# Output projection in seven half-size block products instead of eight

## The chip, the cores and the metric

The kernel runs on one core of one Trainium2 chip. The metric is the device time of one execution in microseconds (us). TensorE (PE in the profile, its weight loads PEld) multiplies, VectorE (DVE), ScalarE (ACT) and GpSimd (POOL) work on tiles in the on-chip memory SBUF and in the accumulators PSUM, SyncE (SP) issues most DMAs. A tile has 128 partitions; "128x544" is 544 numbers in each.

## The reference

One layer of a decoder for a prompt of 1024 tokens and 64 sample tokens, 1088 in all, with 1024 features. The part around the change is:

```python
merged = g_r * (o_r @ lp["w_br_rwkv"]) + g_p * (o_p @ lp["w_br_pool"])
x = x + gt * (merged @ lp["w_out"])
sh, sc, gt = ada_mod(c, lp["w_ada_mlp"], lp["b_ada_mlp"])
h = rms_norm(x, lp["norm_mlp"]) * (1 + sc) + sh
x = x + gt * (jnp.square(jax.nn.relu(h @ lp["w_ff1"])) @ lp["w_ff2"])
```

`w_out` is 1024 x 1024. All data is float32. The gate `gt` has one value for each feature of the prompt, and one for each feature and each of the eight sample sequences.

## The kernel before, in words

Everything is kept with features in partitions and tokens in columns: eight row blocks of 128 features by 1088 columns. The columns are cut into two halves of 544 (`HF`) and four quarters of 272 (`HQ`). A float32 operand is split into a rounded part (`hi`, written by ScalarE) and what is left of it (`lo` = source - `hi`, a subtraction on VectorE or GpSimd); `mm3` then makes three matmuls, `hi*hi`, `hi*lo` and `lo*hi`, into one accumulator. Weights come as halves of a row block, 128x512, and go through `halves` (L236 for `whi`, L237 for `wlo`, which alternates between VectorE and GpSimd).

Three stages matter here. In the **merge stage** eight jobs `or_job(m)` (36 matmuls of 362 or 364 columns each) multiply by `w_br_rwkv`; VectorE multiplies each PSUM result into the gate tile `t` (L1569), L1573 adds the pooling branch `u` (on GpSimd for m < 4, on VectorE above), and L1576 and L1577 split the merged row block into `hi` and `lo` halves, tiles `mr`. In the **output projection** sixteen jobs `out_job(m, i)`, one for each row block m and column half i, make 48 matmuls of 272 columns each, first the eight of the left half, then the eight of the right; each job has two fresh PSUM banks (`mm`, four exist), which VectorE reads once each: `residual` (L2132) multiplies by the gate and adds to the residual row `xr[m]`, a tile of the pool `hx`; in the last quarter the 64 sample columns go through `ns` (L2135) and a GpSimd addition (L2137). Then **the channel mixer** begins, whose first products need `norm2(0)`, the normed left half. Its parts are the squares (ScalarE), their sums (L1620), a matmul with ones, `rms`, the scaling L1635 and `parts` (L1606, L1607), which splits the result.

Each engine executes its instructions in the order in which they stand in the program. That order comes from `Pace.run`: the back program (the matmuls and what follows them directly) runs ahead, each matmul adding a computed time to a clock, and the side programs `norm2(0)`, `norm2(1)` and `ada` are let in when that clock has passed what their `yield` asks for, or when a condition in `self.done` holds. The tile framework puts the waits: a tile name with a limited number of buffers waits for the readers of the buffer's last use. `behind` copies one column from the tile `self.mark` into a new tile (GpSimd, L1536) before a DMA fills it, so that the DMA stays behind the work on `mark`; `next_row` does so for the rows of `x` that become `xr`.

The channel mixer already makes its products in seven blocks instead of eight (`pair_steps`, `product`).

## Time and profile before

| | us |
|---|---|
| time, median of 3 runs (lowest, highest) | 1586.95 (1586.65, 1593.05) |
| the profiled execution, its own time | 1586.22 |
| its span, first to last instruction | 1584.4 |
| PE busy in the span | 1550.8 (98%) |
| DVE busy | 1088.5 (69%) |
| ACT busy | 754.9 (48%) |
| POOL busy | 354.7 (22%) |
| mean granted TensorE clock | 0.998 |

All times in the trace count from the start of the span. In a row of a timeline the columns are start, time taken, engine, line, operation, output <- inputs, shapes and count, and in brackets the idle time before it with what ended that; successive instructions of one line stand in one row (x2), with their time together. In a row of grouped instructions stand the busy time of all, the mean of one in ns, and the idle time before them. In a table of windows each engine has its busy time and, in brackets, its count of instructions. L207 is the line of every matmul, so matmuls are told apart by their tiles.

### The profile page before, as it was taken

What the parts mean: (1) busy time and instruction counts of PE and PEld (TensorE: products, weight loads), DVE (VectorE), ACT (ScalarE), POOL (GpSimd) and SP (SyncE); (2) the same over time, 40 slices, a digit from 0 to 9 for tenths busy, and PEclk for the clock granted to TensorE, in tenths of its full rate; (3) what the DMA queues carried; (4) which work ended last, traced back from release to release, by engine and by line L of the source; (5) the groups of instructions that cost most, each with busy time, mean ns of one, the idle gap of its engine ahead of it and who ended that gap; (6) DMA issues with size and microseconds to landing.
All of it is one profiled execution on the core that took longest, in us unless ns stands there. A gap on an engine that the chain in (4) does not pass through costs nothing.

```text
span 1584.4 us, 35298 instructions
## 1 busy us (share of the span) xinstructions
PE 1550.8 (98%) x14153; PEld 1448.6 (91%) x14153; DVE 1088.5 (69%) x1868; ACT 754.9 (48%) x1543; POOL 354.7 (22%) x470
## 2 busy tenths in 40 slices
PE   7999999999999999999999999999999999999997
PEld 3899788998898789889989999999999999999997
DVE  4697777698488747557536776777455767786866
ACT  5454354355346434433335665554545765553323
POOL 3300100020002000103313223222233344521221
PEclk9999999999999999999999999999999999999999
DMA  9334322423423344937874466657667865573213
GB/s 340 108 108 156 129 87 88 143 94 133 130 100 109 101 137 153 337 121 278 286 267 149 155 212 209 220 201 266 214 213 284 274 198 187 194 285 132 94 41 113
DMA packets 124627, 279.21 MB, mean 176 GB/s; under 512 B 18112, under 2 KB 32448, under 8 KB 124464
## 3 DMA queue, kind: packets, MB, share of 16 engines
q1 hardware_dynamic: 109152, 228.52, 42.1%
q0 software_dynamic: 9264, 32.22, 6.2%
q10 hardware_dynamic: 6048, 16.23, 3.0%
q8 instruction: 111, 1.82, 0.5%
q14 instruction: 52, 0.43, 0.1%
HBM read 197.95 MB, written 78.95 MB: 175 GB/s over the span
## 4 chain that ended last, share of the span: by engine, by line
PE 82%; DVE 6%; DMA 5%; ACT 3%; issue 3%; POOL 1%; ACTq 0%; SPq 0%; DVEq 0%; POOLq 0%
PE mm L207 34%; PE pr L207 34%; PE w L207 7%; PE wc L207 6%; DMA aw<-in_w_ada_mix 2%; DMA wraw<-in_w_br 1%; DMA wrx<-in_w_out 1%; DVE hx L1938 0%; DMA x<-in_xT 0%; ACT whi L236 0%; DVE hx L1635 0%; DMA sraw<-in_w_in 0%; PE wc L214 0%; DVE e L419 0%; DVE wlo L237 0%
## 5 line engine op out<-in xcount | busy, mean ns | idle before, releaser
L207 PE MATMUL mm<-hx,whi 128*128 128x364 f32 (+1 forms) x1920 | 497.4, 340 | 1.0 <-POOL hx L539 1.0
L207 PEld LDWEIGHTS mm<-hx,whi 128*128 128x128 f32 x1920 | 332.1, 188 | 33.1 <-issue 17.5
L207 PE MATMUL pr<-mr,whi 128*128 128x272 f32 x1792 | 337.5, 288 | 0.2 <-DVE hx L1938 0.2
L207 PE MATMUL mm<-hx,wlo 128*128 128x364 f32 (+1 forms) x960 | 315.1, 328 | 0.0
L207 PEld LDWEIGHTS pr<-mr,whi 128*128 128x128 f32 x1792 | 280.5, 188 | 2.2 <-issue 2.1
L207 PE MATMUL pr<-mr,wlo 128*128 128x272 f32 x896 | 257.4, 287 | 0.0
L207 PEld LDWEIGHTS mm<-hx,wlo 128*128 128x128 f32 x960 | 180.6, 188 | 0.3 <-DVE wlo L237 0.2
L207 PE MATMUL pr<-hx,whi 128*128 128x272 f32 x896 | 170.7, 289 | 0.3 <-ACT hid L1742 0.3
L207 PEld LDWEIGHTS pr<-mr,wlo 128*128 128x128 f32 x896 | 168.8, 188 | 0.0
L207 PE MATMUL mm<-mr,whi 128*128 128x272 f32 (+5 forms) x736 | 152.5, 302 | 0.0
L236 ACT ACTIVATE whi<-wraw 128x512 fp32r<-128x512 f32 x127 | 79.8, 628 | 138.8 <-PE mm L207 41.5
L207 PEld LDWEIGHTS pr<-hx,whi 128*128 128x128 f32 x896 | 140.7, 189 | 1.4 <-issue 0.8
L236 ACT ACTIVATE whi<-wr 128x512 fp32r<-128x512 f32 x138 | 86.4, 628 | 111.8 <-PE pr L207 81.1
L207 PE MATMUL pr<-hx,wlo 128*128 128x272 f32 x448 | 129.2, 288 | 0.0
L237 DVE TENSOR_TENSOR wlo<-wraw,whi 128x512 fp32r<-128x512 f32 x117 | 84.9, 725 | 56.5 <-ACT whi L236 56.3
L207 PEld LDWEIGHTS mm<-mr,whi 128*128 128x128 f32 x736 | 119.1, 188 | 3.2 <-issue 2.7
L207 PE MATMUL mm<-mr,wlo 128*128 128x272 f32 (+5 forms) x368 | 110.2, 300 | 0.0
L237 DVE TENSOR_TENSOR wlo<-wr,whi 128x512 fp32r<-128x512 f32 x103 | 76.8, 748 | 14.8 <-ACT whi L236 14.6
L207 PE MATMUL pr<-t,whi 128*128 128x272 f32 x448 | 85.0, 288 | 0.0
L207 PEld LDWEIGHTS pr<-hx,wlo 128*128 128x128 f32 x448 | 84.3, 188 | 0.0
L594 DVE TENSOR_TENSOR px<-mm,rb 128x298 f32<-128x298 f32 (+2 forms) x100 | 50.5, 508 | 34.5 <-PE mm L207 33.9
L237 POOL TENSOR_TENSOR wlo<-wrx,whi 128x512 fp32r<-128x512 f32 x31 | 42.6, 1376 | 139.7 <-ACT whi L236 135.3
(494 smaller groups left out, 2864.4 us busy)
## 6 DMA issues: line engine op xcount, KB each, us to landing
wr<-in_w_ff SPq DMA_DIRECT2D x137, 256.0 KB, 3.4
hid<-d_ch POOLq DMA_DIRECT2D x72, 272.0 KB, 3.7
wraw<-in_w_in SPq DMA_DIRECT2D x62, 256.0 KB, 2.9
d_ch<-hx SPq DMA_DIRECT2D x52, 272.0 KB, 3.9
hid<-in_w_ada_mlp SPq DMA_DIRECT2D x24, 512.0 KB, 6.2
d_th<-px SPq DMA_DIRECT2D x22, 544.0 KB, 3.1
wt<-d_x SPq DMA_DIRECT2D x20, 544.0 KB, 4.6
wraw<-in_w_ff SPq DMA_DIRECT2D x36, 256.0 KB, 3.0
```

The lines of the kernel that those rows point to most:

```text
L207: return self.nc.tensor.matmul(out, lhsT, rhs, **kw)
L236: nc.scalar.activation(hi, raw, AF.Copy)
L237: (nc.gpsimd if pool else nc.vector).tensor_tensor(lo, raw, hi.bitcast(F32), op=ALU.subtract)
L594: self.nc.vector.tensor_tensor(out, ps[:, :m], self.rb[:, c0:c0 + m], op=ALU.mult)
```

## The change

The eight products of 2 x 2 blocks (weights and merged activations each cut in halves of their 1024 features and of their tokens) become seven, each a product of a sum of weight blocks and a sum of activation blocks. With B11, B12 the left and right token halves of the merged blocks m = 0 to 3, and B21, B22 those of m = 4 to 7, the seven activation operands are B11, B21, B22, t1 = B12 - B11, t2 = B22 - t1, t3 = t2 - B11 and t4 = B21 - t2. A product has four row blocks j, a step (c, j) is 24 matmuls of 272 columns, and the 28 steps of `out_steps` have 672 matmuls where the sixteen jobs had 768.

The accumulators are kept over several products: step (1, j) opens two banks O[j], and (6, j), (7, j) and (4, j) add to them; (5, j) opens two again, to which (3, j) adds; the four steps of product 2 share one pair, O[4], from the tag `w`. After every step `residual` (L2237) adds what the two banks hold, times the gate, to half of a residual row: 56 reads where there were 32.

The sums: `or_job` makes t1 on GpSimd (L1588) for m < 4; for m > 3 it subtracts in place t2 and t4 (L1598, L1599; GpSimd for m = 4 to 6, VectorE for 7); L1607 makes t3 in eight subtractions on GpSimd, taking `hi` and `lo` of B11 away from t2 in turn. Each is split by `halve` (L1539, L1540). Weight sums are made on GpSimd in `prep` (two subtractions for c = 6, one addition for c = 5, an addition and a subtraction for c = 3: 20 in all). There are 36 loads of w_out halves instead of 32, and 28 splits instead of 32.

`norm2(0)` takes its rows in the order in which they are finished, which is now before the last eight steps, (5, *) and (3, *), and its scaling (L1739) of six of the rows takes its factor from a copy (`behind_mark`, L1706 and L1707, GpSimd) that follows the row named by `mark`; four of its eight remainders (L1702) are on GpSimd instead of one. `next_row` runs two steps behind instead of five. Outside this stretch the constant table is loaded in three parts instead of two, with part of it freed after the first phase.

```diff
-        mg = [[], []]
...
+        Bq, mid, late = {}, {}, {}
+        def halve(c, k, src, place, pool=False):
+            hi, lo = Bq[c, k] = place()
+            nc.scalar.activation(hi, src, AF.Copy)
+            (nc.gpsimd if pool else nc.vector).tensor_tensor(lo, src, hi.bitcast(F32), op=ALU.subtract)
         def behind(x):
...
-            m = step - 5
+            m = step - SHIFT
...
             def after():
-                t = S["t"]
-                (nc.vector if m > 3 else nc.gpsimd).tensor_tensor(t, t, S["u"], op=ALU.add)
-                hi, lo = zip(*[MR() for _ in range(2)])
-                for i, s in enumerate(split):
-                    nc.scalar.activation(hi[i], t[:, s], AF.Copy)
-                    nc.vector.tensor_tensor(lo[i], t[:, s], hi[i].bitcast(F32), op=ALU.subtract)
-                mg[0].append(hi)
-                mg[1].append(lo)
-                self.mark = t
+                t, k = S["t"], m % 4
+                a, b = t[:, :HF], t[:, HF:]
+                for c in split if m == 7 else (slice(0, NT),):
+                    (nc.vector if m > 3 else nc.gpsimd).tensor_tensor(t[:, c], t[:, c], S["u"][:, c], op=ALU.add)
+                if m < 4:
+                    halve("11", k, a, MR)
+                    x = mid[k] = p.tile([P, HF], F32, tag="wr2", bufs=5, name=self.nm("mid"))
+                    nc.gpsimd.tensor_tensor(x, b, a, op=ALU.subtract)
+                    halve("t1", k, x, MR)
+                    self.mark = x
+                else:
+                    halve("21", k, a, MR)
+                    halve("22", k, b, MR)
+                    self.mark = Bq["22", k][0].bitcast(F32)
                 next_row(m)
+                if m > 3:
+                    eng, x = nc.gpsimd if m < 7 else nc.vector, mid[k]
+                    eng.tensor_tensor(b, b, x, op=ALU.subtract)
+                    eng.tensor_tensor(a, a, b, op=ALU.subtract)
+                    late[k] = a, b
+                if m == 7:
+                    for k in range(4):
+                        halve("t2", k, late[k][1], HXP)
+                    for k in range(4):
+                        b, (hi, lo) = late[k][1], Bq["11", k]
+                        for x in (hi, lo):
+                            nc.gpsimd.tensor_tensor(b, b, x.bitcast(F32), op=ALU.subtract)
                 self.done.add(("or", m + 4))
             return Job([io["w_br"][m][:, 0:512]], begin, after=after, xs=lambda: orr, tags=TG)
...
-        def out_job(m, i):
-            return Job([io["w_out"][m][:, h * 512:(h + 1) * 512] for h in range(2)], lambda: self.residual(self.xr[m], gt[:, m, :]), QH[i],
-                       ("mm", "mm"), lambda: out_done(m, i), lambda: mg)
+        def out_steps():
+            A = lambda m, h: io["w_out"][m][:, h * 512:(h + 1) * 512]
+            D, O = [{} for _ in range(4)], {}
+            sub = lambda o, x, y: nc.gpsimd.tensor_tensor(o, x, y, op=ALU.subtract)
+            add = lambda o, x, y: nc.gpsimd.tensor_tensor(o, x, y, op=ALU.add)
+            def raw(j, key, m, h):
+                self.nr += 1
+                t = D[j][key] = self.raw(self.nr % 7 == 6) if self.nr % 7 in (3, 6) else p.tile([P, 512], F32, tag="wr2", bufs=5, name=self.nm("wr2"))
+                nc.sync.dma_start(t, A(m, h))
+                return t
+            def prep(c, j):
+                d = D[j]
+                def go():
+                    if c < 3:
+                        t = self.raw(self.nw % 2)
+                        nc.sync.dma_start(t, A(j, c - 1))
+                        return self.halves(t, False)
+                    if c == 6:
+                        x, y, z = raw(j, "a", j, 0), raw(j, "b", j + 4, 0), raw(j, "c", j + 4, 1)
+                        sub(y, x, y)
+                        sub(x, z, y)
+                        return self.halves(x, False)
+                    if c == 7:
+                        return self.halves(d["b"], True)
+                    if c == 4:
+                        return self.halves(d["c"], False)
+                    if c == 5:
+                        y, z = raw(j, "b", j + 4, 0), raw(j, "c", j + 4, 1)
+                        add(y, y, z)
+                        return self.halves(y, False)
+                    x, z = raw(j, "a", j, 0), raw(j, "e", j, 1)
+                    add(x, x, z)
+                    sub(x, x, d["b"])
+                    return self.halves(x, False)
+                return go
+            def run(c, j):
+                key, m, i = {1: ("11", j, 0), 2: ("21", j, 0), 6: ("t2", j, 1), 7: ("t3", j + 4, 1), 4: ("t4", j + 4, 0),
+                             5: ("t1", j + 4, 1), 3: ("22", j, 1)}[c]
+                def go(w):
+                    if c in (1, 5) or (c, j) == (2, 0):
+                        tag = "w" if (c, j) in ((2, 0), (1, 2), (5, 1)) else "mm"
+                        O[4 if c == 2 else j] = [self.ps(tag) for _ in range(2)]
+                    ps = O[4 if c == 2 else j]
+                    for q in range(2):
+                        o, s = ps[q][:, :HQ], slice(q * HQ, (q + 1) * HQ)
+                        for k in range(4):
+                            xh, xl = Bq[key, k]
+                            self.mm(o, w[k][0], xh[:, s], start=k == 0 and c in (1, 2, 5), stop=False, skip_group_check=True)
+                            self.mm(o, w[k][0], xl[:, s], start=False, stop=False, skip_group_check=True)
+                            self.mm(o, w[k][1], xh[:, s], start=False, stop=k == 3, skip_group_check=True)
+                            yield
+                        self.residual(self.xr[m], gt[:, m, :])(i * HF + q * HQ, HQ, o)
+                    self.mark = self.xr[m]
+                    next_row(len(self.xr) + SHIFT)
+                    if c == 2 and j == 0:
+                        for k in range(4):
+                            halve("t3", k, late[k][1], HXP)
+                    if c == 2 and j == 3:
+                        for k in range(4):
+                            halve("t4", k, late[k][0], MR)
+                    self.done.add(("out", m, 2 if c == 1 else 3 if c in (6, 7) else i))
+                return go
+            two = lambda c, a: [(c, a), (c, a + 1)]
+            seq = [(1, 0), (2, 0), (1, 1), (2, 1)] + two(2, 2)
+            for a in (0, 2):
+                seq += (two(1, 2) if a else []) + two(6, a) + two(7, a) + two(4, a)
+            for a in (0, 2):
+                seq += two(5, a) + two(3, a)
+            return [(prep(c, j), run(c, j)) for c, j in seq]
...
+        def behind_mark(kb):
+            t = p.tile([P, 1], F32, tag="g3", bufs=8, name=self.nm("g3"))
+            nc.gpsimd.tensor_copy(t, self.mark[:, 0:1])
+            nc.gpsimd.tensor_copy(t, g2[:, kb, 0:1])
...
+            for n, m in enumerate((4, 5, 0, 1, 6, 7, 2, 3) if i else (0, 1, 4, 5, 2, 3, 6, 7)):
...
+                yield lambda: ("out", m, i) in self.done and (m > 3 or i or ("out", m, 2) in self.done)
...
-                for kb in (k, k + 4):
+                for kb in (2 * k, 2 * k + 1) if i == 0 else (k, k + 4):
...
-                        nc.vector.scalar_tensor_tensor(x[kb], x[kb], g2[:, kb, 0:1], r, op0=ALU.mult, op1=ALU.mult)
+                        nc.vector.scalar_tensor_tensor(x[kb], x[kb], behind_mark(kb) if kb in TIED else g2[:, kb, 0:1], r, op0=ALU.mult, op1=ALU.mult)
...
-                        parts(kb // 4, k, x[kb], kb == 7)
+                        parts(kb // 4, kb % 4, x[kb], kb in POOLK)
...
+        def out():
+            for _, run in osteps:
+                yield from run(made.pop(0))
+                more()
...
-        for i in range(2):
-            outs = [out_job(m, i) for m in range(8)]
...
-            for j in outs[0 if i else 2:]:
-                order += U(j)
...
+                yield from out()
...
+TIED = (2, 3, 4, 5, 6, 7)
+POOLK = (1, 3, 5, 7)
+SHIFT = 2
```

On VectorE, at the end of the merge stage and in the first steps of the projection, this stood before (`t_1274` is the last merged block, `mr` its halves, `hx` left of the arrow the residual rows, `mm` a bank of a job):

```order
L1577 TENSOR_TENSOR mr_1283_9425<-t_1274_9371,mr_1283_9425 128x544
L237 TENSOR_TENSOR wlo_1293_9470<-wraw_1291_9467,whi_1292_9469 128x512
L2132 SCALAR_TENSOR_TENSOR hx_1262_9306<-mm_1285_9433,gt1_8920,hx_1262_9306 128x272
L2132 SCALAR_TENSOR_TENSOR hx_1262_9306<-mm_1286_9434,gt1_8920,hx_1262_9306 128x272
L2132 SCALAR_TENSOR_TENSOR hx_1273_9368<-mm_1294_9473,gt1_8920,hx_1273_9368 128x272
L2132 SCALAR_TENSOR_TENSOR hx_1273_9368<-mm_1295_9474,gt1_8920,hx_1273_9368 128x272
```

and this stands at the same place now (`hx_1292` to `hx_1295` are the remainders of t2, `t_1281` the last merged block, `w_1306` and `w_1307` the pair of banks of product 2, `mm_1318` and `mm_1319` those of step (1, 1), `wlo_1305` the weight remainder of (1, 1); `hx_1235` and `hx_1247` are residual rows 0 and 1):

```order
L1540 TENSOR_TENSOR hx_1292_9461<-t_1248_9204,hx_1292_9461 128x544
L1540 TENSOR_TENSOR hx_1293_9464<-t_1259_9268,hx_1293_9464 128x544
L1598 TENSOR_TENSOR t_1281_9396<-t_1281_9396,mid_1245_9196 128x544
L1540 TENSOR_TENSOR hx_1294_9467<-t_1270_9332,hx_1294_9467 128x544
L2237 SCALAR_TENSOR_TENSOR hx_1235_9137<-w_1307_9527,gt1_8922,hx_1235_9137 128x272
L237 TENSOR_TENSOR wlo_1288_9445<-wrx_1286_9442,whi_1287_9444 128x512
L1599 TENSOR_TENSOR t_1281_9396<-t_1281_9396 128x544
L237 TENSOR_TENSOR wlo_1305_9523<-wraw_1303_9520,whi_1304_9522 128x512
L2237 SCALAR_TENSOR_TENSOR hx_1247_9201<-mm_1318_9581,gt1_8922,hx_1247_9201 128x272
L1540 TENSOR_TENSOR hx_1295_9470<-t_1281_9396,hx_1295_9470 128x544
L2237 SCALAR_TENSOR_TENSOR hx_1247_9201<-mm_1319_9582,gt1_8922,hx_1247_9201 128x272
L2237 SCALAR_TENSOR_TENSOR hx_1235_9137<-w_1306_9526,gt1_8922,hx_1235_9137 128x272
```

The read of `w_1306`, which step (2, 1) needs free, is the last of these rows; eight operations on two SBUF tiles and three reads of other banks stand ahead of it in these rows.

On GpSimd, at the same place, before:

```order
L237 TENSOR_TENSOR wlo_1281_9420<-wrx_1279_9417,whi_1280_9419 128x512
L1536 COPY hx_1284_9430<-t_1274_9371 128x1
L1536 COPY hid_1289_9440<-t_1274_9371 128x1
L1536 COPY hid_1290_9443<-t_1274_9371 128x1
L1536 COPY hid_1296_9499<-t_1274_9371 128x1
L1559 DMA hx_1284_9430<-in_xT 128x1088
```

and now (`wr2` are weight sums for product 6, `t_1248`, `t_1259`, `t_1270` and `t_1281` are t2 becoming t3, `hx_1302` is residual row 4 and `hx_1235` residual row 0):

```order
L1568 DMA hx_1291_9456<-in_xT 128x1088
L1622 TENSOR_TENSOR wr2_1326_9651<-wr2_1325_9649,wr2_1326_9651 128x512
L1607 TENSOR_TENSOR t_1248_9204<-t_1248_9204,mr_1215_9041 128x544
L1607 TENSOR_TENSOR t_1259_9268<-t_1259_9268,mr_1221_9068 128x544
L1545 COPY hx_1302_9517<-hx_1235_9137 128x1
L1607 TENSOR_TENSOR t_1270_9332<-t_1270_9332,mr_1232_9129 128x544
L1607 TENSOR_TENSOR t_1248_9204<-t_1248_9204,mr_1215_9041 128x544
```

The copy that opens residual row 4 reads a column of residual row 0 and stands behind the weight sum and the first two subtractions for t3; the next write of residual row 0, the last row of the VectorE list above, has to come after it.

On VectorE, at the scaling of `norm2(0)`, before (`mm_1383` and `mm_1394` are banks of jobs of the right half):

```order
L1635 SCALAR_TENSOR_TENSOR hx_1284_9430<-hx_1284_9430,g2_8921,t_1389_10138 128x544
L1635 SCALAR_TENSOR_TENSOR hx_1332_9738<-hx_1332_9738,g2_8921,t_1389_10138 128x544
L1635 SCALAR_TENSOR_TENSOR hx_1304_9543<-hx_1304_9543,g2_8921,t_1389_10138 128x544
L1635 SCALAR_TENSOR_TENSOR hx_1347_9830<-hx_1347_9830,g2_8921,t_1389_10138 128x544
L2132 SCALAR_TENSOR_TENSOR hx_1273_9368<-mm_1394_10157,gt1_8920,hx_1273_9368 128x272
L2132 SCALAR_TENSOR_TENSOR hx_1273_9368<-mm_1395_10158,gt1_8920,hx_1273_9368 128x208
```

and now (`mm_1440` and `mm_1441` are the banks of step (5, 2)):

```order
L1739 SCALAR_TENSOR_TENSOR hx_1258_9263<-hx_1258_9263,g3_1434_10497,t_1418_10379 128x544
L1723 TENSOR_TENSOR t_1188_8926<-t_1188_8926,t_1432_10470 128x544
L1702 TENSOR_TENSOR hx_1426_10441<-hx_1235_9137,hx_1426_10441 128x544
L2237 SCALAR_TENSOR_TENSOR hx_1302_9517<-mm_1440_10521,gt1_8922,hx_1302_9517 128x272
L237 TENSOR_TENSOR wlo_1439_10518<-wrx_1436_10511,whi_1438_10517 128x512
L1739 SCALAR_TENSOR_TENSOR hx_1269_9327<-hx_1269_9327,g3_1443_10536,t_1418_10379 128x544
L1739 SCALAR_TENSOR_TENSOR hx_1280_9391<-hx_1280_9391,g3_1445_10557,t_1418_10379 128x544
L1739 SCALAR_TENSOR_TENSOR hx_1291_9456<-hx_1291_9456,g3_1453_10592,t_1418_10379 128x544
L1739 SCALAR_TENSOR_TENSOR hx_1302_9517<-hx_1302_9517,g3_1455_10613,t_1418_10379 128x544
L2237 SCALAR_TENSOR_TENSOR hx_1302_9517<-mm_1441_10522,gt1_8922,hx_1302_9517 128x208
L2240 TENSOR_TENSOR ns_338<-mm_1441_10522,gt1_8922 128x64
```

The eight scalings stood in one piece (the last four are shown), and no read of a bank among them; now the last reads of the banks of (5, 2), which (3, 2) adds to next, stand behind five of them, a sum of squares and two remainders.

## The prediction

> **What bounds the kernel now.** I read the page's busy shares first, then its chain of waits, then TensorE's waits in the stretch of the change, then windows of its stages.

> ```profile
> PE 1550.8 (98%) x14153; PEld 1448.6 (91%) x14153; DVE 1088.5 (69%) x1868; ACT 754.9 (48%) x1543; POOL 354.7 (22%) x470
> PE 82%; DVE 6%; DMA 5%; ACT 3%; issue 3%; POOL 1%; ACTq 0%; SPq 0%; DVEq 0%; POOLq 0%
> PE pr L207 <- ACT hid L1742: 0.3, 1, 0.3
> 733.00:765.00 32.00, 32.00 (x195) 32.00 (x194) 28.68 (x37) 11.91 (x21) 14.01 (x10) 1.00 0.77 271
> 765.00:876.00 111.00, 110.88 (x890) 104.33 (x890) 54.69 (x95) 43.29 (x72) 32.36 (x39) 1.00 0.69 239
> ```

> The first two rows are of the whole kernel: TensorE is busy 98% of the span and makes up 82% of the chain. The third is all that TensorE waits for between 700 and 960 us: 0.3 us. The last two are windows: the merge stage (from 733 to 765) and the output projection with its tail. TensorE has no idle time in either, so a matmul less is 1:1 time saved, and a wait more is 1:1 time lost; nothing else has to give. VectorE, though, is busy 28.68 of 32 us in the merge stage, and GpSimd 14.01. That is where the change puts its work.

> **The matmuls removed.** The pace of a 272-column matmul is read from a piece of the projection in which TensorE's timeline has 28 successive groups of three:

> ```profile
> 765.32 0.42 PE L207 MATMUL mm<-mr,whi 128*128 128x272 f32 x2
> 861.73 0.41 PE L207 MATMUL mm<-mr,whi 128*128 128x272 f32 x2
> 871.84 0.42 PE L207 MATMUL mm<-mr,whi 128*128 128x272 f32 x2
> ```

> From 861.73 to 871.84 are 27 groups, 0.3744 us each, 0.1248 a matmul. 768 - 672 = 96 matmuls are **-12.0 us**. A step of 24 is 2.99 us. The projection begins at 765.32; up to there TensorE has the same work as before.

> **What two engines can't do at once.** The new sums are GpSimd and VectorE operations on two SBUF tiles. The next rows are VectorE's and GpSimd's timelines in the merge stage and at `norm2(0)`, and two groups.

> ```profile
> 733.86 3.69 DVE L1577 TENSOR_TENSOR mr<-t,mr 128x544 fp32r<-128x544 f32 x2
> 750.43 1.35 DVE L1577 TENSOR_TENSOR mr<-t,mr 128x544 fp32r<-128x544 f32 x2
> 755.55 0.52 DVE L1569 SCALAR_TENSOR_TENSOR t<-t,mm 128x362 f32<-128x362 f32 x1
> 756.55 1.39 DVE L1573 TENSOR_TENSOR t<-t,hid 128x1088 f32<-128x1088 f32 x1
> 733.68 2.64 POOL L1573 TENSOR_TENSOR t<-t,hid 128x1088 f32<-128x1088 f32 x1 [2.34 <-DMA hid<-d_th]
> 755.44 1.34 POOL L237 TENSOR_TENSOR wlo<-wrx,whi 128x512 fp32r<-128x512 f32 x1 [6.37 <-ACT whi L236]
> 849.70 3.50 DVE L1607 TENSOR_TENSOR hx<-hx,hx 128x544 fp32r<-128x544 f32 x2
> 849.51 1.30 POOL L237 TENSOR_TENSOR wlo<-wrx,whi 128x512 fp32r<-128x512 f32 x1
> 850.77 1.84 POOL L1607 TENSOR_TENSOR hx<-hx,hx 128x544 fp32r<-128x544 f32 x1
> L1812 POOL TENSOR_TENSOR hx<-hx,hx 128x544 f32<-128x544 f32 x1 | 1.4, 1367 | 0.7 <-DVE hid L1810 0.7
> L2132 DVE SCALAR_TENSOR_TENSOR hx<-mm,gt,hx 128x272 f32<-128x272 f32 x24 | 11.9, 496 | 24.0 <-PE mm L207 22.2 <-issue 1.8
> ```

> Two remainders on VectorE take 1.35 us where GpSimd is quiet (750.43), and 3.69 where GpSimd's sum of 2.64 began just ahead of them (733.68): 3.69 - 1.35 = 2.34, nearly all of the GpSimd operation. A VectorE operation on a PSUM bank and one tile (755.55) takes its usual 0.52 although GpSimd works from 755.44 on. So a GpSimd sum and a VectorE operation on two tiles go one after the other, and their times add; PSUM reads go beside. At 849.51 they alternate: GpSimd to 850.81, VectorE's first remainder, GpSimd's second operation to 852.61, VectorE's second to 853.20, 0.59 after it. I use 0.58 us for a VectorE operation of 512 or 544 in such alternation (0.635 alone, from 1.35 for two with their overlap), twice that, 1.15, for 1088, 0.45 for a PSUM read (0.52 less the overlap with its neighbour); 1.30, 1.37 and 2.54 for GpSimd's of 512, 544 and 1088. [...]

> **A, step (2, 0).** Between 733.25 and the weight remainder of step (2, 0), the program orders now have on VectorE 19 operations of 512 or 544 and three of 1088, and on GpSimd three of 1088, nine of 544 (mids and late sums; none before) and two of 512. On the common path that is 19 x 0.58 + 3 x 1.15 = 14.5 and 3 x 2.54 + 9 x 1.37 + 2 x 1.30 = 22.5: 37 us, to 770.3; moments in which both wait for ScalarE's halves or for the last merge products, 2.2 by my walk through the orders, make it 772.5. TensorE wants that remainder at 765.32 + 2.99 + 0.25 = 768.6. The fourth block's own remainder comes after two more VectorE operations, a GpSimd sum and a ScalarE half, 775.7, where TensorE, 3.9 late, would want it at 773.6. I take **A = 6.0**. Bounds: 0, if the two engines don't exclude each other here, and 7.2, if the three GpSimd sums of 1088 take 2.95 as in this row:

> ```profile
> 738.95 2.95 POOL L1573 TENSOR_TENSOR t<-t,hid 128x1088 f32<-128x1088 f32 x1 [2.63 <-DVE t L1569]
> ```

> **B, step (2, 1).** Product 2 has one pair of banks, and (2, 1) can't begin before VectorE has read `w_1306`. In VectorE's order this read stands behind nine operations on two tiles and five bank reads counted from 775.7, and it waits for the GpSimd copy that opens residual row 4, behind t3's first subtractions. GpSimd has in that time a weight sum and six of the eight t3 subtractions ready. On the common path: 1.30 + 6 x 1.37 = 9.5, 9 x 0.58 = 5.2, and 1.8 for four reads that nothing covers: to 792. TensorE, through (2, 0) and (1, 1), is there at 768.3 + 6 + 6.0 = 780.3. **B = 11**; without exclusion VectorE alone needs 9 x 0.635 + 6 x 0.45 = 8.4, to 784.1, a wait of 3.7; the upper bound is 11.8. Behind the read on VectorE stand t3's remainders and the next weight remainder, but with product 2 waiting they only come as late as TensorE does.

> **C, step (6, 1).** Its weight remainder stands behind five halves of t3 and t4, two bank reads and two GpSimd remainders: 1.5, between 0 and 2.4.

> **D, the tail.** `norm2(0)` had eight jobs, 8 x 48 x 0.1248 = 47.9 us, to hide behind; now eight steps, 23.9.

> ```profile
> 836.50 6.68 DVE L1635 SCALAR_TENSOR_TENSOR hx<-hx,g,t 128x544 f32<-128x544 f32 x8
> ```

> Before, the left half ended at 765.32 + 47.9 = 813.2 and the scalings began 23.3 later. With shorter leads now, and GpSimd's weight sums waiting for their loads, I put them 12.9 after E, the end of (4, 3). From there to the last read of the bank pair of (5, 2) VectorE has eleven operations on two tiles (6.4) and six bank reads (2.2), and at least three of GpSimd's remainders and sums come in between (3.7), as at 849.70, where two remainders took 3.50: E + 25.2. (3, 2) wants the second bank at E + 6.5 x 2.99 = E + 19.4. That is 5.8, and the banks of (5, 3) follow closely: **D = 6**. Lower bound 0 (without exclusion the read comes at about E + 19), upper 8. Nothing of it returns later, since TensorE is full up to the end.

> **At nothing.** 56 bank reads for 32: 24 x 0.496 = 11.9 us of VectorE, in steps in which it was busy 54.69 of 111 us; uncovered, they are in A to D. Four loads more of w_out, four splits fewer: loads land 3.1 us after their issue and are asked for steps ahead:

> ```profile
> wrx<-in_w_out SPq DMA_DIRECT2D x16, 256.0 KB, 3.1
> ```

> The constant table in three loads is worth 0.5 either way at the start, next to weight loads on all queues; I take 0.

> **The sum.** -12.0 + 6.0 + 11 + 1.5 + 6 = +12.5 on the profiled run's own 1586.22: 1598.7. Its time stands 0.73 below the median of the runs, so **1599**. With the lower bounds together (3.7) 1578.7, with the upper (29.4) 1604.4.

> **Rivals.** *R1, queue order alone.* The exclusion costs nothing here because GpSimd's sums fall into VectorE's PSUM reads: three reads of L1569 in each of eight jobs, at 0.45, are 11 us. A and C vanish, B falls to 3.7, D to half, 3: -12.0 + 6.7, **1581.7**. Against it: the GpSimd work is twice those 11 us, and row 733.86 shows it hitting the remainders. *R2, the other side: the full gain.* The late sums are not on the path: if the common path has done the remainder of (2, 0) by 768.6, and the bank read of (2, 0) by the end of (1, 1), TensorE goes through. It decides at 35.4 us of common work from 733.25, where I count 37: within 5%. With VectorE's operations at their undisturbed place and D hidden by eight full steps, -12.0: **1574.9**. For it speaks that I may have counted sums before the remainder that lose the race for the path; against it, that B needs nine more. *R3, a slow restart.* TensorE never stood still for 6 or 11 us here. If its clock falls in such gaps and needs about a step to come back, each step-length of 2.99 at half speed loses 1.5; after A, B and D that is 4.5: **1603.9**. Two windows at the start bear on it:

> ```profile
> 4.00:8.00 4.00, 0.30 (x2) 0.33 (x2) 1.64 (x7) 3.11 (x4) 1.03 (x2) 1.00 1.01 356
> 8.00:12.00 4.00, 0.92 (x4) 0.39 (x5) 1.93 (x2) 1.67 (x3) 2.60 (x4) 1.00 1.10 310
> ```

> The granted clock reads 1.00 with TensorE nearly idle, so the column speaks against it as far as it can show. [...]

> **How the numbers follow.** The forecast 0.51, R1 0.22, R2 0.16, R3 0.11. The forecast's own range, with the bounds of B and D moved half, is 1591 to 1606. About 0.5% (1579.0 and 1594.9) is what a measurement here can tell from no change. Faster: R2 and 0.03 of R1, 0.19. Slower: 0.47 of the forecast and R3, 0.58. Same: 0.19 of R1 and 0.04 of the forecast, 0.23. The range for 8 in 10 takes in R1 and R3 and leaves out R2 and a little above: 1577 to 1608.

> **What would show it.** A: in the window of the merge stage GpSimd busy 22 us or more and a TensorE wait on a VectorE remainder of (2, 0). B: a wait of TensorE on a residual read at L2237 of `w`, about 11 us, the longest of the projection. D: waits on L2237 with VectorE's scalings L1739 ahead. The projection, from its first matmul to the channel mixer's first, would be 95.9 - 12.0 + 24.5, about 108 us. Steps of 2.99 right after the waits speak against R3, of 4 or more for it. TensorE waits of under 3 us in the whole stretch would make the forecast wrong, and R2 right; so would VectorE remainders of 0.68 beside a busy GpSimd.

## The result, and the profile after

The changed kernel is slower: 1612.99 us median (1608.45 to 1614.86, 6 runs) against 1590.74 (1586.65 to 1594.48, 6 runs) for the kernel before, a ratio of 1.0138 with a 95% interval of 1.0114 to 1.0162. The forecast, slower by 12.5 us, had the direction and about half the size; the time lies above its range. The profiled execution took 1610.72 us, its span is 1608.9, 24.5 more than the span before.

The page of the changed kernel has TensorE as busy as before, in a longer span, and GpSimd 62 us busier:

```profile
PE 1551.8 (96%) x14057; PEld 1446.3 (90%) x14057; DVE 1136.0 (71%) x1920; ACT 759.0 (47%) x1551; POOL 416.4 (26%) x520
```

96 matmuls fewer, and 1.0 us more of busy time: so many of the remaining ones took longer. TensorE's waits between 700 and 960 us (total, times, longest) were one row of 0.3 us; now they are ten, of which these six make 21.3 of 22.9 us:

```profile
PE w L207 <- DVE hx L2237: 8.0, 3, 5.8
PE w L207 <- DVE wlo L237: 5.0, 1, 5.0
PE mm L207 <- DVE ns L2240: 4.7, 2, 3.3
PE pr L207 <- ACT whi L236: 1.7, 1, 1.7
PE mm L207 <- DVE hx L2237: 1.1, 2, 0.8
PE wc L207 <- DVE t L1723: 0.8, 1, 0.8
```

Windows of the merge stage and of the first steps. The column after POOL is the granted clock; in the kernel before it reads 1.00 in both:

```profile
733.00:765.00 32.00, 32.00 (x195) 32.00 (x194) 29.46 (x32) 10.30 (x17) 25.24 (x20) 1.00 0.89 320
765.00:805.00 40.00, 26.82 (x170) 25.32 (x172) 37.01 (x41) 13.44 (x24) 31.61 (x29) 0.83 0.52 180
```

In the second TensorE is busy 26.8 of 40 us, with its clock at 0.83 on the average. GpSimd was busy 14.01 us in the merge stage and is now busy 25.24.

**Where the 24.5 us are.** From the first matmul of the projection (765.32 before, 766.46 now) to the 4000th matmul counted from the end, which is the same in both (1048.89 and 1073.77), it was 283.57 us and is 307.31: 23.74 longer, so the 96 matmuls were bought with 35.7. I took the distances between the starts of successive matmuls, each less the usual distance of its form, and sorted them: distances with idle time in them are 25.8 us more than before (the 22.9 of waits, and 2.9 with which the matmuls right after a wait start more slowly), those while the clock stands at half are 8.6, all others 1.3. Ahead of the projection it was 1.1 later already, all of it by 700 us, and 0.4 come back behind the 4000th matmul from the end: 24.5.

### The profile page after: what moved, and what is told of

Its sections match the earlier page's. It is cut to its first block, busy times and chain, and to the rows that moved or that the text cites. A ratio compares the mean times of both kernels' runs of the same rounds, so it can differ in the third digit from the quotient of the medians.

```text
span 1608.9 us, 35227 instructions
## 1 busy us (share of the span) xinstructions
PE 1551.8 (96%) x14057; PEld 1446.3 (90%) x14057; DVE 1136.0 (71%) x1920; ACT 759.0 (47%) x1551; POOL 416.4 (26%) x520
## 4 chain that ended last, share of the span: by engine, by line
PE 79%; DVE 8%; DMA 6%; issue 3%; ACT 3%; POOL 2%; SPq 0%; DVEq 0%; ACTq 0%; POOLq 0%
PE pr L207 34%; PE mm L207 31%; PE w L207 7%; PE wc L207 6%; DMA aw<-in_w_ada_mix 2%; DMA wraw<-in_w_br 1%; DMA wr<-in_w_out 1%; DVE wlo L237 1%; POOL t L1607 1%; POOL wr L1622 1%; DMA hid<-in_w_ada_mlp 0%; DMA sraw<-in_w_in 0%; DVE hx L2048 0%; DVE hx L1739 0%; DMA x<-in_xT 0%
## 5 line engine op out<-in xcount | busy, mean ns | idle before, releaser
L207 PE MATMUL mm<-hx,whi 128*128 128x364 f32 (+2 forms) x2016 | 515.8, 338 | 0.4 <-POOL hx L539 0.4
L207 PEld LDWEIGHTS mm<-hx,whi 128*128 128x128 f32 x2016 | 347.2, 188 | 33.2 <-issue 18.1
L207 PE MATMUL pr<-mr,whi 128*128 128x272 f32 x1792 | 338.8, 288 | 1.9 <-ACT whi L236 1.7
L207 PE MATMUL mm<-hx,wlo 128*128 128x364 f32 (+2 forms) x1008 | 329.0, 326 | 0.5 <-DVE wlo L237 0.5
L207 PEld LDWEIGHTS pr<-mr,whi 128*128 128x128 f32 x1792 | 281.7, 189 | 4.0 <-ACT whi L236 1.9
L207 PE MATMUL pr<-mr,wlo 128*128 128x272 f32 x896 | 258.1, 288 | 0.4 <-DVE wlo L237 0.4
L207 PEld LDWEIGHTS mm<-hx,wlo 128*128 128x128 f32 x1008 | 189.6, 188 | 1.0 <-DVE wlo L237 0.9
L207 PE MATMUL pr<-hx,whi 128*128 128x272 f32 x896 | 172.5, 291 | 0.0
L207 PEld LDWEIGHTS pr<-mr,wlo 128*128 128x128 f32 x896 | 169.5, 189 | 0.6 <-DVE wlo L237 0.6
L236 ACT ACTIVATE whi<-wr 128x512 fp32r<-128x512 f32 x152 | 95.1, 628 | 138.7 <-PE pr L207 85.1
L207 PEld LDWEIGHTS pr<-hx,whi 128*128 128x128 f32 x896 | 142.2, 191 | 0.9 <-issue 0.8
L236 ACT ACTIVATE whi<-wraw 128x512 fp32r<-128x512 f32 x118 | 74.1, 628 | 126.9 <-PE mm L207 47.1
L207 PE MATMUL pr<-hx,wlo 128*128 128x272 f32 x448 | 130.3, 291 | 0.0
L237 DVE TENSOR_TENSOR wlo<-wraw,whi 128x512 fp32r<-128x512 f32 x108 | 84.3, 781 | 39.7 <-ACT whi L236 37.0
L237 DVE TENSOR_TENSOR wlo<-wr,whi 128x512 fp32r<-128x512 f32 x113 | 84.4, 749 | 23.0 <-ACT whi L236 23.0
L207 PE MATMUL mm<-mr,whi 128*128 128x272 f32 (+5 forms) x416 | 93.7, 315 | 5.8 <-DVE ns L2240 4.7
L207 PE MATMUL pr<-t,whi 128*128 128x272 f32 x448 | 85.0, 288 | 0.0
L207 PEld LDWEIGHTS pr<-hx,wlo 128*128 128x128 f32 x448 | 85.0, 190 | 0.0
L207 PEld LDWEIGHTS mm<-mr,whi 128*128 128x128 f32 x416 | 70.1, 191 | 8.0 <-DVE ns L2240 5.1
L207 PEld LDWEIGHTS pr<-t,whi 128*128 128x128 f32 x448 | 70.1, 188 | 0.8 <-issue 0.8
L1971 POOL DMA_DIRECT2D hid<-d_ch x72 | 38.9, 544 | 105.9 <-DVE mr L1973 69.5
## 6 DMA issues: line engine op xcount, KB each, us to landing
wr<-in_w_ff SPq DMA_DIRECT2D x137, 256.0 KB, 3.3
wraw<-in_w_in SPq DMA_DIRECT2D x62, 256.0 KB, 2.9
wraw<-in_w_ff SPq DMA_DIRECT2D x36, 256.0 KB, 3.3
```

What stands on the lines that cost most here:

```text
L207: return self.nc.tensor.matmul(out, lhsT, rhs, **kw)
L236: nc.scalar.activation(hi, raw, AF.Copy)
L237: (nc.gpsimd if pool else nc.vector).tensor_tensor(lo, raw, hi.bitcast(F32), op=ALU.subtract)
L1971: nc.gpsimd.dma_start(x, self.d_ch[c][j])
```

## The experiments

Where a run is given by its span alone, there was one run of that kernel. Runs of the kernel before lie between 1585.2 and 1595.5 us, so such a run is read by its waits and not by its span.

**Does GpSimd's work alone make TensorE wait?** Ten subtractions of no use were put into the kernel before, where the changed kernel has its first ten activation sums:

```diff
                 self.mark = t
+                for c in range(1 if m < 4 else 2 if m < 7 else 0):
+                    x = p.tile([P, 512], F32, tag="wr2", bufs=5, name=self.nm("idle"))
+                    nc.gpsimd.tensor_tensor(x, t[:, 512:1024], t[:, :512], op=ALU.subtract)
                 next_row(m)
```

> The kernel before with ten subtractions of no use (128x512) on GpSimd in the merge stage, at the places where the changed kernel makes its first ten activation sums, and nothing that waits for them. Exclusion theory: they delay VectorE's remainders by up to 13 us of GpSimd time less what slack VectorE had (3.3 of 32 us in the stage, and some at its end): TensorE waits for remainders at the start of the projection, 3 to 7 us with restarts, and a half-clock stretch if the wait passes about 2 us; 1587 becomes 1591 to 1596. Rival (GpSimd's work is free to the others): no wait, no change.

1599.03 us (1596.76 to 1605.12, 7 runs), ratio 1.0061 (1.0036 to 1.0086): some 10 us for work that nobody waits for, more than the 4 to 9 expected. The timelines of VectorE and GpSimd in that run show how:

```profile
760.85 3.10 DVE L1577 TENSOR_TENSOR mr<-t,mr 128x544 fp32r<-128x544 f32 x2
759.96 3.41 POOL L1583 TENSOR_TENSOR idle<-t 128x512 f32<-128x512 f32 x2 [1.23 <-DVE t L1573]
772.11 2.90 DVE L1573 TENSOR_TENSOR t<-t,hid 128x1088 f32<-128x1088 f32 x1
772.57 1.29 POOL L237 TENSOR_TENSOR wlo<-wrx,whi 128x512 fp32r<-128x512 f32 x1
```

Two remainders that took 1.35 us in the kernel before (at 758.90) take 3.10 beside two of the added subtractions (L1583). VectorE's last addition of the merge stage began at 767.22 and took 1.39 us in the kernel before; here it comes at 772.11 and takes 2.90 beside a GpSimd operation, and TensorE's wait of 2.5 us for the last `hi`, which ScalarE makes from it, is the longest of that run's projection. The rival, GpSimd as free work, falls. GpSimd's own weight remainders came later as well (this one at 772.57 instead of 766.12), and TensorE waited 0.6 us in the merge stage for one of them; how the 10 us divide between VectorE held off and GpSimd's own queue, this run doesn't tell.

**The sums on VectorE instead.** The 18 sums on GpSimd (t1, t2, t4, t3) become VectorE's:

```diff
-                    nc.gpsimd.tensor_tensor(x, b, a, op=ALU.subtract)
+                    nc.vector.tensor_tensor(x, b, a, op=ALU.subtract)
...
-                    eng, x = nc.gpsimd if m < 7 else nc.vector, mid[k]
+                    eng, x = nc.vector, mid[k]
...
-                            nc.gpsimd.tensor_tensor(b, b, x.bitcast(F32), op=ALU.subtract)
+                            nc.vector.tensor_tensor(b, b, x.bitcast(F32), op=ALU.subtract)
```

> All 18 new activation sums that the changed kernel makes on GpSimd (4 for t1, 6 for t2 and t4, 8 for t3) are made on VectorE instead. Exclusion theory (a GpSimd sum and a VectorE operation on two SBUF tiles go one after the other): each sum costs the common path 0.64 us instead of 1.37, ten of them ahead of step (2, 0): TensorE's wait there falls from 5.0 us to under 1, the waits on the banks of product 2 from 8.0 to under 3, the half-clock stretches between 773 and 794 us go, and the span falls from 1608.9 to about 1592 to 1597. Rival (VectorE is simply too long, GpSimd's work is free beside it): VectorE gets 18 x 0.64 = 11.5 us more where it is already busy 33 of 35 us, the waits grow by 5 to 11 us and the span is 1614 to 1622.

Waits and windows of that run:

```profile
PE w L207 <- DVE hx L2237: 5.4, 3, 2.5
PE w L207 <- DVE wlo L237: 2.7, 1, 2.7
...
733.00:765.00 32.00, 32.00 (x195) 32.00 (x194) 31.64 (x39) 10.30 (x17) 15.20 (x13) 1.00 0.89 323
765.00:805.00 40.00, 31.74 (x205) 28.91 (x205) 39.06 (x61) 16.83 (x28) 13.91 (x18) 0.87 0.57 201
```

The waits at product 2 fell from 13.0 to 8.1 us though VectorE had 18 operations more: that speaks for the exclusion and against the rival, by which they would have grown. But they didn't fall to 4. VectorE is now busy 31.64 of 32 and 39.06 of 40 us: its own length has become the limit. At the 4000th matmul from the end the profiled execution is 4.45 us ahead of the changed kernel's (1069.32 against 1073.77). At its end nothing is left of that (span 1608.6): 3.3 us went in the last stage, in waits that the changed kernel doesn't have there; why they came is open. The time is 1608.99 us (1607.08 to 1610.35, 4 runs), ratio 1.0115 (1.0098 to 1.0132), an interval that overlaps the changed kernel's; the expected span of 1592 to 1597 was missed.

**All sums left out.** t1 to t4 are split from plain blocks (the result is then another one):

```diff
-                    x = mid[k] = p.tile([P, HF], F32, tag="wr2", bufs=5, name=self.nm("mid"))
-                    nc.gpsimd.tensor_tensor(x, b, a, op=ALU.subtract)
-                    halve("t1", k, x, MR)
-                    self.mark = x
+                    halve("t1", k, b, MR)
+                    self.mark = t
...
-                    eng.tensor_tensor(b, b, x, op=ALU.subtract)
-                    eng.tensor_tensor(a, a, b, op=ALU.subtract)
...
-                            nc.gpsimd.tensor_tensor(b, b, x.bitcast(F32), op=ALU.subtract)
```

> The changed kernel without its activation sums: t1 to t4 are split from the plain blocks, so the 20 sums are left out and nothing else (the result is then another one). If the sums cause the waits at steps (2, 0) and (2, 1), both fall to under 1.5 us together and the clock is full up to the tail: span 1589 to 1593. If the shared bank pair of product 2 or the order of the queues causes them without the sums, at least 4 us of waits on that pair stay: span 1597 or more. The waits of the tail (5.8 us from 879 to 892) stay in both.

The expectation was wrong by 9 us: the span is 1602.0. The waits for the banks of product 2 are gone, which is against the second side of it; but others stand in their place, which is against the first. The waits of TensorE between 760 and 870, and the ScalarE row behind the second:

```profile
PE mm L207 <- DVE wlo L237: 4.4, 3, 1.8
PE w L207 <- ACT whi L236: 3.9, 1, 3.9
785.54 0.63 ACT L236 ACTIVATE whi<-wraw 128x512 fp32r<-128x512 f32 x1 [8.62 <-DMA wraw<-in_w_out]
777.37 0.38 SPq L1628 DMA_DIRECT2D wraw<-in_w_out  x1
771.11 6.17 SPq L343 DMA_DIRECT2D hid<-in_w_ada_mlp  x4
```

The load of w_out that (2, 2) needs was issued at 777.37, behind four loads of `w_ada_mlp` on SP's queue, and landed at about 785.5. The changed kernel comes to (2, 2) only at 795.12 and shows no wait for a load there. So without the sums the waits on the banks go, but that frees only some 6 of the 14 us of waits in this stretch (8.3 are left).

**Is it the shared bank pair?** Product 2 got a second pair:

```diff
-                    if c in (1, 5) or (c, j) == (2, 0):
-                        tag = "w" if (c, j) in ((2, 0), (1, 2), (5, 1)) else "mm"
+                    if c in (1, 5) or c == 2:
+                        tag = "wc" if c == 2 and j % 2 else "w" if c == 2 or (c, j) in ((1, 2), (5, 1)) else "mm"
```

> The changed kernel with a second pair of banks for product 2: steps (2, 1) and (2, 3) use the pair of the tag wc, so (2, 1) needs no read of the banks of (2, 0). VectorE's order up to that read is unchanged. If VectorE's late work as such is the cause (my theory), (2, 1) now waits for its weight remainder, two rows ahead of the bank reads, which VectorE ended at 786.4 in the changed kernel against 783.5 for TensorE: a wait of about 3 us; the waits of (2, 1) to (2, 3) fall from 8.0 to between 3 and 5, the span to 1602 to 1606. If the shared pair is the cause, they fall to under 1.5 and the span to 1597 to 1600.

```profile
PE w L207 <- DVE wlo L237: 5.2, 1, 5.2
PE mm L207 <- ACT whi L236: 4.4, 1, 4.4
PE wc L207 <- DVE wlo L237: 3.3, 1, 3.3
PE w L207 <- DVE hx L2237: 1.1, 1, 1.1
```

Step (2, 1) now begins right after (1, 1) and waits for nothing: its wait of 5.8 us for the bank is gone, and its weight remainder is there in time, so the expected wait of 3 us at this step isn't there either. The lateness shows further on: 1.1 at (2, 2) for a bank, 3.3 at (2, 3) for its weight remainder, and 4.4 at (6, 0) for a weight. From (2, 1) to (2, 3) the waits are 4.4 us instead of 8.0, as the first theory had it in sum; the span stayed (1608.3 for 1602 to 1606 expected). So the shared pair decides at which step TensorE waits, and a second one does not make VectorE's late work earlier.

**Everything on VectorE.** The sums of activations and weights, the remainders of the normed left half and two bank pairs together; then the additions L1584 of m < 4 too; then the same with one pair:

```diff
-POOLK = (1, 3, 5, 7)
+POOLK = ()
...
-                        sub(y, x, y)
-                        sub(x, z, y)
+                        nc.vector.tensor_tensor(y, x, y, op=ALU.subtract)
+                        nc.vector.tensor_tensor(x, z, y, op=ALU.subtract)
...
-                    (nc.vector if m > 3 else nc.gpsimd).tensor_tensor(t[:, c], t[:, c], S["u"][:, c], op=ALU.add)
+                    nc.vector.tensor_tensor(t[:, c], t[:, c], S["u"][:, c], op=ALU.add)
```

> The changed kernel with all new sums, of activations and weights, and the remainders of the normed left half on VectorE, and with the second pair of banks for product 2. Theory: waits at product 2 under 4 us in all, in the tail under 4, one or two half-clock stretches instead of five; the span falls by 12 to 18 us to 1591 to 1597, still slower than the kernel before. Rival (VectorE too long): waits of 20 us and more, span above 1605.

> The kernel of e8 with the four additions of the pooling branch (1088 columns, 2.54 us each) on VectorE as well (1.22 each). VectorE was busy 31.6 of 32 and 38.6 of 40 us there from 733 to 805. Exclusion theory: the common path gets 4 x 1.3 = 5 us shorter; TensorE's waits between 766 and 805 (13.5 us with their restarts) fall by 3 to 5, the span to 1600 to 1603. Rival (VectorE's own length counts): it gets 4.9 us more, the waits rise by that, span 1608 or more.

> The kernel of e9 with the one shared bank pair of the changed kernel for product 2. If the second pair is worth nothing as e6 says, within 2 us of e9, and the pair wc left to the other work; if the shared pair costs a wait of its own once VectorE is early, 2 to 5 us slower than e9 with waits on L2237 or its like at w.

1604.49 us (ratio 1.0087, 1.0061 to 1.0113), 1601.49 (1.0080, 1.0054 to 1.0106) and 1604.98 (1.0091, 1.0057 to 1.0125). All three lie below the changed kernel's 1.0138 (1.0114 to 1.0162), the first two with intervals that end just below it, the last with one that overlaps it, and none is as fast as the kernel before. In the first the waits at product 2 are 4.8 (under 4 expected) and those for banks in the tail 3.1, but 4.5 came up at product 6. The expected spans of the first (1591 to 1597, measured 1605.6) and the second (1600 to 1603, measured 1603.2) were not reached. Among themselves the three can't be told apart, so a second bank pair is worth nothing that shows here. In the first, VectorE's window from 765 to 805 was

```profile
765.00:805.00 40.00, 30.74 (x207) 26.38 (x206) 38.59 (x65) 16.36 (x28) 10.32 (x15) 0.91 0.70 236
```

38.59 of 40: again full. The waits of the second there were 10.8 us against 9.3 in the first, not less: moving the four additions gave (2, 0) its weight in time and the next bank read (9.2 us) took over, at (2, 3). The fall of the waits by 3 to 5 us that was expected isn't there.

**The tail.** The weight sums of products 5 and 3 and the four remainders of `norm2(0)` go to VectorE, nothing else:

```diff
-                        add(y, y, z)
+                        nc.vector.tensor_tensor(y, y, z, op=ALU.add)
...
-                    add(x, x, z)
-                    sub(x, x, d["b"])
+                    nc.vector.tensor_tensor(x, x, z, op=ALU.add)
+                    nc.vector.tensor_tensor(x, x, d["b"], op=ALU.subtract)
...
-POOLK = (1, 3, 5, 7)
+POOLK = ()
```

> The changed kernel with the tail's GpSimd sums on VectorE: the weight sums of products 5 and 3 (12 of 128x512) and the remainders of rows 1, 3, 5 and 7 of the normed left half. Exclusion theory: each costs the common path 0.64 instead of 1.3 us; TensorE's waits between 870 and 900 us (5.8 for the banks of (5, 2) and (5, 3), 0.8 for the sum of squares) fall to under 3.5, the waits at product 2 stay. Rival (VectorE's own queue is what is too long there): they grow to 8 or more.

```profile
PE mm L207 <- DVE ns L2239: 3.1, 2, 2.2
PE wc L214 <- DVE rt L381: 1.7, 1, 1.7
```

Between 870 and 900 us the waits were 6.6 us in the changed kernel (4.7, 1.1 and 0.8) and are 3.1, under the 3.5 expected; all 3.1 are for banks, instead of 5.8. Just ahead of it, at 867.65, a wait grew from 0.3 to 1.7. The span is 1604.1. So here, too, GpSimd's operations were in VectorE's way, for about half of the waits on banks.

**Is the clock a cost of its own?** Matmuls of no use fill the two gaps:

```diff
+                    if (c, j) in WARMUP:
+                        n, tag = WARMUP[c, j]
+                        d = self.ps(tag)[:, :HQ] if tag else ps[0][:, :HQ]
+                        for r in range(n):
+                            self.nc.tensor.matmul(d, w[0][0], Bq[key, 0][0][:, 0:HQ], start=True, stop=True, skip_group_check=True)
...
+WARMUP = {(2, 0): (40, None), (2, 1): (46, "wc")}
```

> The changed kernel with 40 matmuls of no use ahead of step (2, 0) (into the bank that the step then overwrites) and 46 ahead of step (2, 1) (into a free bank), about 5.0 and 5.8 us, the length of the waits there; the waits themselves stay, TensorE is busy in them. Slow-clock theory (TensorE's clock is halved after a stretch in which it was mostly idle): the two half-clock stretches of 6.8 us each go, steps (2, 0) and (2, 1) take 3.0 us instead of 5.0 and 4.4, the span falls by 3 to 4.5 us to 1604.5 to 1606. Rival (the matmuls there are slow because VectorE and GpSimd crowd SBUF): they stay slow, the span stays at 1609 or above.

```profile
775.60:782.80 7.20, 6.11 (x46) 5.90 (x47) 7.20 (x13) 4.09 (x8) 4.70 (x5) 1.00 0.71 234
782.80:792.20 9.40, 9.25 (x72) 8.81 (x70) 3.45 (x7) 1.18 (x2) 9.40 (x8) 1.00 0.39 134
802.84 0.79 PE L207 MATMUL w<-mr,whi 128*128 128x272 f32 x2 [10.70 <-DVE hx L2242]
```

In the first two windows, VectorE busy all through the one and GpSimd through the other, the clock stays at 1.00 and the steps run at full pace (three matmuls in 0.37 us from 778.32 on); the rival (a crowded SBUF slows the matmuls) falls. The time didn't fall by 3 to 4.5 us but rose, to 1618.15 (ratio 1.018, 1.016 to 1.020): (2, 2) waited 10.7 us for a bank, unfilled, and the clock reads 0.50 from 797.2 to 807.4. That the added matmuls moved VectorE's bank reads behind other work in its order is my reading; no run isolates it. So the filled gaps show what slows the matmuls, and not what a full clock is worth in time.

A gap put into the projection of the kernel before, which has none there, and six short ones:

```diff
+            if (m, i) in GAPS:
+                d = T()[:, :HF]
+                nc.scalar.activation(d, self.xr[m][:, :HF], AF.Copy)
+                for _ in range(GAPS[m, i] - 1):
+                    nc.scalar.activation(d, d, AF.Copy)
+                self.nc.tensor.matmul(self.ps("wc")[:, 0:5], d[:, 0:128], self.kc("one0")[:, :5], start=True, stop=True)
...
+GAPS = {(3, 0): 11}
```

> The kernel before, with one gap put into TensorE's work: a matmul of 5 columns after job (3, 0) waits for a chain of 11 ScalarE copies, so that TensorE stands still for about 8 us. Slow-clock theory: the clock records show a half-clock stretch of one or two times 3.4 us, matmuls right after the gap take 0.43 instead of 0.29 us, and the loss is the gap plus 1.5 to 4 us. Rival (a gap costs its own length): no half-clock record, loss equal to the gap.

> The kernel before with six short gaps instead of a long one: after each of the jobs (1, 0) to (6, 0) a matmul of 5 columns waits for one ScalarE copy of the finished row, about 1.3 us of idle TensorE each, 6 us and more apart. Slow-clock theory with a threshold (the changed kernel's clock records fall after stretches of 3.4 us in which TensorE was idle for 1.9 us or more, not after ones with 1.4 to 1.7): no half-clock record in the projection, loss equal to the gaps within 1 us. Rival (each gap costs a slow restart of its own): 1 to 2 us per gap beyond it, 6 or more in all.

```profile
PE wc L1599 <- ACT t L1598: 13.1, 1, 13.1
804.90:810.30 5.40, 5.40 (x25) 4.27 (x29) 0.00 (x0) 0.00 (x0) 0.00 (x0) 0.50 0.00 0
```

The long gap came out at 13.1 us instead of 8. From the projection's first matmul to the 4000th from the end the run is 16.2 us longer than the kernel before (299.73 against 283.57), so 3.1 beyond the gap, and the clock reads 0.50 up to 810.4 and 1.00 after it. With the six gaps (one `GAPS` entry of 1 for each of m = 1 to 6), five were 1.3 us and one, by a late copy, 4.2. These are windows of one short gap and of what follows the long one:

```profile
774.00:777.40 3.40, 2.07 (x17) 1.85 (x16) 1.00 (x2) 1.06 (x2) 0.71 (x2) 1.00 0.92 321
797.54:800.95 3.41, 3.39 (x15) 3.39 (x16) 1.34 (x1) 0.52 (x1) 1.29 (x1) 0.50 0.88 269
```

Only the 4.2 us gap had a half-clock stretch behind it, none of the five short ones. The expectation, no half clock at all and a loss within 1 us of the gaps, was for six short ones. The same stretch is 15.6 us longer (299.20 against 283.57), with 10.8 of gaps; 1.6 of the difference is half clock, the rest (about 3 us, with the added matmuls themselves in it) is not sorted further. The rival's 6 us and more beyond the gaps aren't there.

## Why the prediction was right or wrong

Term by term, in us:

| step of the prediction | predicted | measured |
|---|---|---|
| 96 matmuls fewer | -12.0 | -12.0 at the unchanged pace |
| A, weight remainder of (2, 0) | +6.0 | +5.0 |
| B, banks of product 2, (2, 1) to (2, 3) | +11 | +8.0 (5.8, 0.7, 1.6) |
| C, step (6, 1) | +1.5 | 0 |
| D, tail, banks of (5, 2) and (5, 3) | +6 | +5.8 |
| other waits | 0 | +4.1 |
| slower starts after waits | 0 | +2.9 |
| half clock | 0 (R3: +4.5) | +8.6 |
| everything else in the stretch | 0 | +1.3 |

**Right: the matmuls, the places of A, B and D and their cause.** The waits that the forecast had priced, 24.5, came out at 18.8; (6, 1) didn't wait at all. VectorE, GpSimd and TensorE at the start of the projection, for A:

```profile
769.99 4.25 DVE L1584 TENSOR_TENSOR t<-t,hid 128x544 f32<-128x544 f32 x1
775.81 0.71 DVE L1584 TENSOR_TENSOR t<-t,hid 128x544 f32<-128x544 f32 x1
769.81 1.34 POOL L1598 TENSOR_TENSOR t<-t,mid 128x544 f32<-128x544 f32 x1
771.11 1.26 POOL L1622 TENSOR_TENSOR wr<-wr,wr 128x512 f32<-128x512 f32 x1
772.33 1.32 POOL L1599 TENSOR_TENSOR t<-t 128x544 f32<-128x544 f32 x1
774.90 0.59 PE L207 MATMUL w<-mr,wlo 128*128 128x272 f32 x1 [5.03 <-DVE wlo L237]
```

The same addition takes 0.71 us alone and 4.25 when three GpSimd operations run through it, to 773.65; the weight remainder of (2, 0) stands right behind it, and TensorE gets it at 774.90. My walk let the engines take turns, which is the wrong picture here: VectorE's addition, begun at 769.99, ended at 774.24, behind all three. A's size is in part luck: the sum had the weight remainder at 772.5 and a second wait, for the fourth block's own remainder, up to 775.7. The first came 2.3 us later than that, and of the second 0.5 is left (two matmuls in 1.16 us at 776.65 instead of 0.66), because step (2, 0) then ran at half clock; in the run with the filled gaps, at full clock, it was 1.0.

B ends with the read of `w_1306`, as the prediction had it. Rows of GpSimd, VectorE and TensorE:

```profile
785.78 0.64 POOL L1545 COPY hx<-hx 128x1 f32<-128x1 f32 x1
788.63 0.48 DVE L2237 SCALAR_TENSOR_TENSOR hx<-w,gt,hx 128x272 f32<-128x272 f32 x1
789.26 0.79 PE L207 MATMUL w<-mr,whi 128*128 128x272 f32 x2 [5.78 <-DVE hx L2237]
```

The copy that opens residual row 4 was done at 786.42, so it was VectorE's own order that ended last. B is the term of the sum that was most off: 792 less 780.3 is 11.7, taken as 11, and the wait at (2, 1) was 5.8. The read ended 3 us earlier than 792: the sum had put six of GpSimd's subtractions for t3 ahead of it, and two had run by 785.84, with three more from 786.38 to 790.79. TensorE arrived 3 us later than the sum had it (783.5): the projection began 1.1 later, and step (2, 0) ran at half clock. Its later arrival hid part of the wait. D is the read of the second bank of (5, 2) behind four scalings, as the order showed:

```profile
880.22 3.97 DVE L1739 SCALAR_TENSOR_TENSOR hx<-hx,g,t 128x544 f32<-128x544 f32 x4
884.46 0.21 DVE L2240 TENSOR_TENSOR ns<-mm,gt 128x64 f32<-128x64 f32 x1
884.72 0.52 PE L207 MATMUL mm<-mr,whi 128*128 128x272 f32 x2 [3.29 <-DVE ns L2240]
```

**Wrong: the clock.** The step that failed is in R3: "The granted clock reads 1.00 with TensorE nearly idle, so the column speaks against it as far as it can show." The two windows were at the kernel's start. The trace has no clock record before 17.27 us, and the column reads 1.00 where there is none. I took that for a full clock, gave R3 a chance of 0.11 and put the clock at nothing in the forecast's sum. The trace of the kernel before held what was needed, at its two ends. These are its 16 matmuls `wc<-aw,sT` from 11.44 to 17.6 us, the 48 of the same shape from 25 us on (behind the bar their busy time together in us, then the mean of one in ns), and two windows at its end:

```profile
L207 PE MATMUL wc<-aw,sT 128*32 128x512 f32 x16 | 6.2, 1026 | 3.1 <-DMA aw<-in_w_ada_mix 3.1
L207 PE MATMUL wc<-aw,sT 128*32 128x512 f32 x48 | 7.6, 603 | 0.5 <-DMA aw<-in_w_ada_mix 0.5
1573.75:1577.16 3.41, 1.56 (x11) 1.16 (x10) 2.79 (x8) 1.44 (x5) 0.65 (x2) 1.00 0.46 167
1577.16:1580.57 3.41, 0.00 (x0) 0.00 (x0) 3.22 (x8) 1.28 (x3) 1.79 (x2) 0.50 0.83 290
```

The same matmul took 1026 ns at the start, where the column reads 1.00, and 603 later: it was slow there. And at the end the clock goes to 0.50 after a window in which TensorE was busy for 1.56 of 3.41 us. So that trace did have windows that speak for R3; no later matmul paid for the 0.50 there.

In the changed kernel the clock fell five times between 773 and 951 us. Windows of 3.41 us (one of twice that) before three of these stretches, the first of the stretches, and one window after which the clock didn't fall:

```profile
769.74:773.15 3.41, 0.13 (x2) 0.00 (x0) 3.38 (x2) 0.00 (x0) 3.39 (x4) 1.00 0.62 192
773.15:779.97 6.82, 4.94 (x20) 4.62 (x21) 6.82 (x12) 3.99 (x7) 3.11 (x6) 0.50 0.45 137
878.97:882.38 3.41, 1.74 (x12) 1.55 (x12) 3.33 (x7) 3.18 (x7) 3.41 (x10) 1.00 0.39 136
882.38:885.79 3.41, 1.07 (x8) 1.07 (x9) 3.41 (x5) 3.41 (x6) 3.41 (x3) 1.00 0.00 2
947.23:950.64 3.41, 1.49 (x9) 1.27 (x10) 2.99 (x5) 3.06 (x6) 3.41 (x1) 1.00 0.24 93
```

At half clock three matmuls took 0.68 us (the groups that start at 775.29, 775.97 and 776.65) instead of 0.375. In the clock's place the runs showed 8.6 us, and 2.9 more for slower starts right after waits, which the sum put at nothing too. R3's own price was low as well: it counted three stretches of 1.5 us; there were five, two of them 6.83 us long. R3's half speed and its return after about a step were assumptions of mine, with no row beside them; what was measured is a clock of 0.50 for 3.41 or 6.83 us, behind windows in which TensorE was busy for 0.13, 1.07 or 1.49 of 3.41 us.

The right direction is in part luck. With the priced waits as they came out, 18.8, and nothing else, the sum would have been +6.8 us, less than the 0.5% (8 us) that the prediction called the least that can be told from no change; the terms at nothing, which are the clock, the slower starts, the other waits and the rest, added 16.9. The stretch from the projection's first matmul to the channel mixer's first was to grow from 95.9 to about 108 us; it grew from 110.3 to 126.5, since other matmuls than those of `w_out` run in it, which the 95.9 leaves out.

**Not foreseen:** of the other waits, 2.1 us are in the first products of the channel mixer (947 to 950, for ScalarE's split of a weight and for its remainder), and a half-clock stretch came behind them. No run tells why ScalarE is late there. The others are 0.8, 0.5, 0.4 and 0.3 us; the 0.5 is at (6, 3).

**R1 and R2** fell. R1 had the exclusion cost nothing; with ten subtractions of no use on GpSimd the kernel before took 1599.03 us instead of 1589.07. R2 had the remainder of (2, 0) done by 768.6; TensorE went on with it at 774.90.

## What to carry to other kernels

Work that was moved to GpSimd was not free here beside a VectorE that reads two SBUF tiles (an addition of 0.71 us took 4.25 beside three GpSimd operations): count both engines' such operations on one line, with GpSimd's at their own, longer times, and compare that line with the time that TensorE gives. Where TensorE is the bound and never waits, price a new wait at more than its length: here the work after the waits of 5.0, 5.8 and 3.3 us ran at a clock of 0.50, and half clock was 8.6 of the 35.7 us that this change lost. Before a column of a profile is used against a rival, compare the durations of one shape of matmul in the same window. And a saving of matmuls in a stage where VectorE is already 90% busy (28.68 of 32 us) has to pay for its sums in that stage, not in the kernel's mean of 69%.

## What the runs showed of the hardware that was not expected

VectorE's addition at 769.99 took 4.25 us instead of 0.71 while three GpSimd operations ran in a row, and the other way round: a GpSimd weight sum, 1.26 us at 771.11, took 3.98 at 778.33 while VectorE went through four remainders and sums on two tiles.
